# A hybrid state-space and pooling layer on one core: the z projection moved out of the state-space groups and made from seven block products per pair

## The chip, the cores and the metric

One Trainium2 chip, one of its cores. The metric is the device time of one execution in microseconds (us), as the median of several runs. A lower time is better. All inputs and outputs are fp32 tensors in the chip's memory.

## What is computed

One layer of a streaming encoder, for two request groups that share the weights: one prompt of 512 tokens and 8 samples of 16 tokens, together 640 tokens (`TOK`) with a model width of 1024. The reference, cut to the mixing sub-layer:

```python
u = rms_norm(x, g_pre_mix) * (1 + sc1) + sh1
proj = u @ w_in                                   # 1024 -> 9248
z, xbc, dt_raw, p, gates = jnp.split(proj, [2048, 6144, 6176, 7200], axis=-1)
xbc_c = jax.nn.silu(causal_dwconv(conv_hist, xbc, conv_w, conv_b))
xs, bm, cm = jnp.split(xbc_c, [2048, 3072], axis=-1)
dt = jax.nn.softplus(dt_raw + dt_bias);  a = -jnp.exp(a_log)
y, h_final = ssd_chunked(xs, dt, a, bm, cm, h0)   # 8 groups of 4 heads, state 128
y = y + xs * d_skip
yg = y.reshape(b, L, 2048) * jax.nn.silu(z)
yg = yg * lax.rsqrt(mean(yg * yg over the 256 columns of a group) + EPS)
y_ssd = (yg * g_ssd_norm) @ w_ssd_out
y_pool = multiscale_pool(p) @ w_pool_group * pool_scale
mix = (sigmoid(gate_a) * y_ssd + sigmoid(gate_b) * y_pool) @ w_o
x = x + gt1 * rms_norm(mix, g_post_mix)
```

The channel sub-layer follows: `w_up` (1024 to 4096), a squared ReLU, `w_down`. Inside `ssd_chunked` the decay of position l from position s is exp(min(a_cs[l] - a_cs[s], 0)), masked to s <= l. New states of the recurrence, the convolution and the pooling are outputs too.

## The kernel before

Activations lie transposed, features on the 128 partitions and the 640 tokens along the free dimension. Every large product is made in three fp32r matmuls: an operand is split in a high part (a cast on ACT, `S.copy`) and a low part (the rest, a subtraction on DVE), and hi*hi, lo*hi and hi*lo are added up in PSUM. `split` (lines 119 to 134) does this for one weight block of 128 x 1024, in rings of four `wh` and `wl` buffers. `fmm` (lines 154 to 162) makes one tile of 128 output features: 8 blocks of the inner dimension x 3 terms x 2 token regions, of 256 and of 384 tokens, so 48 matmuls with 320 columns on average, into one of two large PSUM buffers (`big`). Raw weights come in blocks of 1 MB through two `raw` buffers, loaded by SP's queue.

The stages in the order of the program:

- Prologue and pooling: conditioning, u, dt, the pooling branch `p` (tiles `pp`, `ypp`), and the first 2 of 16 gate tiles (`gate`, tiles `pga` and `pgb`; `gate_list`). The pooling branch's result goes to DRAM (`yp_d`), and a gate tile of the second half reads it back (`ypl`), multiplies, and writes `bf_d`. tanh of a gate tile lies in `tA`, the pooled rows in `tB`, two buffers each.
- State-space stage, 8 groups. `proj(g)` makes six tiles: four `px` (two of x, one of B, one of C; each followed by `conv_tile`, the width-4 convolution and its silu, in `L634` to `L646`) and two `pz` (`ztile`: tanh of half z on ACT, `L681`, then (tanh + 1) * z on DVE, `L682`, into `sz`). `ssd(g)` is the recurrence of a group in nine pieces; for each of five token tiles `common(t)` loads decay rows (`ab`, DMA by SP), transposes (`tp`), clamps with `pacs` on DVE (`M`, `L714`), takes four exp on ACT (`L716`, bias `nacs`), and PE makes `py` and `sp`. `sample_t`, `sample_a`, `sample_b` treat the 8 samples (`hTp`, `yo`, `ss`); `finish` multiplies by `sz` and sends `yg_d`; `finish2` sums squares (`ms`). `merge` lays `ssd(g-1)` between the tiles of `proj(g)`; in groups 2 to 5 the conditioning columns that are needed later (`ada`, `L301`, 1 MB of weights a step) lie among them too. `ssd(7)` lies between six gate tiles; eight gate tiles follow.
- Phase B: for each group one row of factors (`rb`) and two tiles (`yg`) are loaded by SP, multiplied (`L913`) and split (`put`, `L187` and `L188`) in `ynh` and `ynl`; then the tiles `pso` of `w_ssd_out`.
- Phase C and the channel sub-layer: `w_o` (`po`), v, then pairs of `w_up` tiles (class `Pair`, tiles `pq` and `pr`) and `w_down` (`pd`, `L1236`). A `Pair` makes two tiles from seven products of half size: the inner dimension, the two output tiles and the tokens (two halves of 320) are halved, sums of blocks are formed on DVE, and each product is 4 inner blocks x 3 terms = 12 matmuls of 320 columns (`L1185`), 84 in all. The first pair is made plainly (`L1169`), 96 matmuls of 320 columns.

The program is written in this order, and a scheduler at build time sets the order of each engine's queue; every queue (PE, ACT, DVE, POOL, and SP for DMA) then runs in order.

Of the kernel before, what the change touches and what calls it, by code (L numbers as in the profile page):

```python
# [60 lines left out]
def tile_hybrid_step(  # L61
# [36 lines left out]
    g_d = dp.tile([2, 9, 1024], F32, name="g_d")  # L98
    v_d = dp.tile([8, 128, 640], F32, name="v_d")
# [49 lines left out]
    PS0 = 256  # L149

    def reg(ps, g):
        return ps[:, 256:512] if g == 0 else ps[:, 512:896]

    def fmm(ps, w, act, ks, first, last, groups=(0, 1)):
        wh, wl = w
        (ah, al) = act
        n = len(ks)
        for i, (kw, ka) in enumerate(ks):
            for j, (ww, aa) in enumerate(((wh, ah), (wh, al), (wl, ah))):
                for g in groups:  # L160
                    T.matmul(reg(ps, g), ww[:, kw, :], aa[g][:, ka, :],  # L161
                             start=first and i == 0 and j == 0, stop=last and i == n - 1 and j == 2)
# [26 lines left out]

    def rsqrt(pool, m, shape, dst, tag):  # L190
# [25 lines left out]


# [12 lines left out]
    nacs = cp.tile([128, NT, 32], F32, name="nacs")  # L230
# [109 lines left out]
    uh, ul = act_views(256)  # L340
# [28 lines left out]
    def ada_cols(b):  # L369
# [213 lines left out]
    def gate(which, f):  # L583
# [5 lines left out]
        with tc.high_priority():  # L589
            S.activation(th, ps[:, PS0:PS0 + 640], AF.Tanh, scale=0.5)  # L590
# [35 lines left out]

    es_a = ExitStack()
    A = es_a.enter_context(tc.tile_pool(name="phaseA", bufs=1, reuse_waits="tile"))
    xcs, szs = {}, {}

    def conv_tile(ps, dst, ci, rc, slot):
        pv = ps[:, PS0:PS0 + 640].rearrange("p (b s) -> p b s", s=16)
# [7 lines left out]
        S.activation(ac, ps[:, PS0:PS0 + 640], AF.Identity, bias=colf[:, CB + ci:CB + ci + 1], scale=colw[:, 96 + ci:97 + ci])  # L640
# [7 lines left out]
    def proj(g):  # L648
# [3 lines left out]
        def xtile(i):  # L652
# [10 lines left out]
            conv_tile(ps, st["xc"][:, i, :], cols[i], st["rc"], i)  # L663

# [680 lines left out]
```

## Time and profile before

| | |
|---|---|
| median of 3 runs | 1366.09 us (1364.56 to 1368.3) |
| the profiled execution | 1366.78 us, its span 1365.0 us |
| PE busy | 1324.6 us, 97% of the span, 8940 matmuls |
| DVE, ACT, POOL busy | 892.8, 569.5, 90.7 us |
| moved by DMA | 192.25 MB, mean 141 GB/s |

A span runs from the first to the last instruction of the profile; what lies around it, 1.8 us here, is in the device time only. Busy time of PE counts overlapping matmuls, so a stage that is 100% busy can still hold short waits: how fast PE really goes is read from the start of one matmul to that of the next, or from the length of a whole tile. The granted clock is TensorE's, where 1.00 is 2.4 GHz and 0.50 is 1.2 GHz.

### The profile page before, as it was taken

What the parts mean: (1) busy time and instruction counts of PE and PEld (TensorE: products, weight loads), DVE (VectorE), ACT (ScalarE), POOL (GpSimd) and SP (SyncE); (2) the same over time, 40 slices, a digit from 0 to 9 for tenths busy, and PEclk for the clock granted to TensorE, in tenths of its full rate; (3) what the DMA queues carried; (4) which work ended last, traced back from release to release, by engine and by line L of the source; (5) the groups of instructions that cost most, each with busy time, mean ns of one, the idle gap of its engine ahead of it and who ended that gap; (6) DMA issues with size and microseconds to landing.
All of it is one profiled execution on the core that took longest, in us unless ns stands there. A gap on an engine that the chain in (4) does not pass through costs nothing.

```text
span 1365.0 us, 22238 instructions
## 1 busy us (share of the span) xinstructions
PE 1324.6 (97%) x8940; PEld 1195.8 (88%) x8940; DVE 892.8 (65%) x1729; ACT 569.5 (42%) x1097; POOL 90.7 (7%) x153
## 2 busy tenths in 40 slices
PE   4999999999999999999998999999999999999997
PEld 3999998878887889989898999779988988988886
DVE  4775667767776879686547333488745756667675
ACT  4444546454545555564334221365441422423331
POOL 0011011010201020102100000011000000000000
PEclk9999999999999999999999999999999999999999
DMA  9744524565546653435367633635212312212151
GB/s 298 224 112 125 157 84 125 148 216 187 167 147 214 181 180 93 130 105 173 103 205 267 211 100 132 216 122 187 93 62 63 104 51 93 93 55 100 62 201 47
DMA packets 134927, 192.25 MB, mean 141 GB/s; under 512 B 8541, under 2 KB 104877, under 8 KB 132776
## 3 DMA queue, kind: packets, MB, share of 16 engines
q1 hardware_dynamic: 123336, 160.96, 36.9%
q0 software_dynamic: 10016, 29.56, 6.9%
q8 instruction: 70, 1.15, 0.3%
q10 hardware_dynamic: 1472, 0.31, 0.1%
q14 instruction: 33, 0.27, 0.1%
HBM read 159.20 MB, written 31.60 MB: 140 GB/s over the span
## 4 chain that ended last, share of the span: by engine, by line
PE 84%; DMA 6%; DVE 4%; issue 3%; ACT 2%; ACTq 0%; POOL 0%; SPq 0%; DVEq 0%; POOLq 0%
PE pd L1236 16%; PE px L161 14%; PE pq L1185 8%; PE pz L161 8%; PE pso L161 8%; PE pga L161 4%; PE pr L1185 3%; PE po L989 3%; PE pp L161 3%; PE py L729 2%; DMA wz<-in_w_in_dram 2%; PE sp L748 1%; PE hTp L783 1%; PE yo L788 1%; PE pq L1169 1%
## 5 line engine op out<-in xcount | busy, mean ns | idle before, releaser
L161 PE MATMUL px<-AH,wh 128*128 128x256 f32 (+1 forms) x512 | 119.1, 314 | 0.0
L161 PE MATMUL px<-AH,wl 128*128 128x256 f32 (+1 forms) x512 | 117.9, 310 | 0.0
L161 PE MATMUL px<-AL,wh 128*128 128x256 f32 (+1 forms) x512 | 117.5, 310 | 0.0
L161 PEld LDWEIGHTS px<-AH,wh 128*128 128x128 f32 x512 | 91.5, 188 | 8.1 <-issue 4.6
L161 PEld LDWEIGHTS px<-AH,wl 128*128 128x128 f32 x512 | 93.0, 188 | 0.3 <-issue 0.3
L161 PEld LDWEIGHTS px<-AL,wh 128*128 128x128 f32 x512 | 93.1, 188 | 0.0
L1254 DVE TENSOR_TENSOR acc<-acc,pd 128x512 f32<-128x512 f32 (+1 forms) x61 | 40.7, 676 | 72.6 <-PE pd L1236 72.6
L1236 PE MATMUL pd<-wl,hh 128*128 128x512 f32 (+1 forms) x223 | 87.8, 394 | 0.2 <-DVE wl L133 0.2
L1236 PE MATMUL pd<-wh,hl 128*128 128x512 f32 (+1 forms) x223 | 87.7, 393 | 0.0
L1236 PE MATMUL pd<-wh,hh 128*128 128x512 f32 (+1 forms) x223 | 85.9, 392 | 0.0
L642 DVE SCALAR_TENSOR_TENSOR ac<-rw,colw,ac 128x640 f32<-128x640 f32 x96 | 84.3, 878 | 2.0 <-ACT ac L640 1.4
L161 PE MATMUL pz<-AH,wh 128*128 128x256 f32 (+1 forms) x256 | 62.4, 320 | 0.0
L161 PE MATMUL pz<-AH,wl 128*128 128x256 f32 (+1 forms) x256 | 61.4, 315 | 0.0
L161 PE MATMUL pz<-AL,wh 128*128 128x256 f32 (+1 forms) x256 | 60.3, 314 | 0.0
L716 ACT ACTIVATE M<-M,nacs 128x128 f32<-128x128 f32 x160 | 52.4, 397 | 17.0 <-DVE M L714 17.0
L161 PE MATMUL pso<-ynh,wh 128*128 128x256 f32 (+1 forms) x256 | 58.3, 309 | 0.0
L161 PE MATMUL pso<-ynh,wl 128*128 128x256 f32 (+1 forms) x256 | 58.3, 309 | 0.0
L161 PE MATMUL pso<-ynl,wh 128*128 128x256 f32 (+1 forms) x256 | 58.3, 309 | 0.0
L161 PEld LDWEIGHTS pz<-AH,wh 128*128 128x128 f32 x256 | 46.0, 188 | 6.8 <-issue 4.9
L1236 PEld LDWEIGHTS pd<-wl,hh 128*128 128x128 f32 x223 | 41.9, 188 | 9.7 <-DVE wl L133 0.6
L1236 PEld LDWEIGHTS pd<-wh,hl 128*128 128x128 f32 x223 | 42.0, 188 | 9.3
L1236 PEld LDWEIGHTS pd<-wh,hh 128*128 128x128 f32 x223 | 41.8, 188 | 8.8
(493 smaller groups left out, 3638.2 us busy)
## 6 DMA issues: line engine op xcount, KB each, us to landing
wada<-in_w_ada_dram SPq DMA_DIRECT2D x24, 1024.0 KB
wu<-in_w_up_dram SPq DMA_DIRECT2D x16, 1024.0 KB
wd<-in_w_down_dram SPq DMA_DIRECT2D x16, 1024.0 KB
ab<-acs_d SPq DMA_DIRECT2D x40, 256.0 KB
wxs<-in_w_in_dram SPq DMA_DIRECT2D x8, 1024.0 KB
wbc<-in_w_in_dram SPq DMA_DIRECT2D x16, 512.0 KB
wz<-in_w_in_dram SPq DMA_DIRECT2D x8, 1024.0 KB
h<-in_state_ssm_dram SPq DMA_DIRECT2D x16, 512.0 KB
```

Of the source, the lines that this page charges most:

```text
L161: T.matmul(reg(ps, g), ww[:, kw, :], aa[g][:, ka, :], start=first and i == 0 and j == 0, stop=last and i == n - 1 and j == 2)
L642: V.scalar_tensor_tensor(a3, rw[:, :, k:k + 16], colw[:, 32 * k + ci:32 * k + ci + 1], a3, ALU.mult, ALU.add)
L716: S.activation(M[:, hh, :], M[:, hh, :], AF.Exp, bias=nacs[:, t, 4 * g + hh:4 * g + hh + 1])
L729: T.matmul(py[64 * j:64 * (j + 1), 128 * qq:128 * (qq + 1)], xr[:, 2 * qq + j, :], M[:, 2 * qq + j, :], start=True, stop=stop)
L748: T.matmul(sp[:, 0:256], bt, xrd, start=True, stop=True)
L783: T.transpose(pt[:, 128 * b:128 * (b + 1)], st["h0"][qq][:, 4 * hb + b, :], ident)
L788: T.matmul(po[32 * c:32 * c + 32, o:o + 128], st["xc"][:, 3, 512 + 32 * c:512 + 32 * c + 32], hT[:, 2 * c + par, :], start=True, stop=True ...
L989: T.matmul(ps[:, HC[half]], aa[:, k, :], ww[:, HC[half]], start=k == 0 and j == 0, stop=k == 7 and j == 2)
L1169: T.matmul(ps[:, 512 * g:512 * g + HT], ww[:, k, :], aa[g][:, k, :], start=k == 0 and j == 0, stop=k == 7 and j == 2)
L1185: T.matmul(dst, ww[:, k, :], aa[:, k, :], start=start and k == 0 and j == 0, stop=stop and k == 3 and j == 2, skip_group_check=True)
L1236: T.matmul(ps, aa[:, k, :], ww[:, cols], start=first and k == 0 and j == 0, stop=last and k == n - 1 and j == 2)
L1254: V.tensor_tensor(acc[t][:, hc], acc[t][:, hc], ps, ALU.add)
```

## The change

- z leaves `proj`. A new class `Seven`, which also replaces `Pair`, makes the 16 z tiles as 8 pairs in a stage of their own between pooling and the state-space groups. For it u lies in two regions of 320 tokens (`HT`), the high and low parts of u are added up again (`uf`), four combinations of its quarters are formed and split (`UH`, `UL`), and four gate tiles are made ahead of the pairs. Each z tile, times tanh + 1 (or, negated, tanh - 1), goes to DRAM (`sz_d`) by POOL's queue, and `start` of a group loads it back by SP's.
- `proj` keeps the four `px` tiles; `ssd(7)` lies between four gate tiles instead of six, and six instead of eight follow.
- The clamp min(., 0) of the decay goes from DVE to ACT: relu of (pacs - ab) in four instructions, then one exp of the negative over all 512 columns. `nacs` goes.
- High and low parts of the pooled rows and of phase B's tiles lie in one row of 640 (`put_flat`): one cast and one subtraction each instead of two.
- The load of `yp_d` in a gate tile goes from SP's queue to POOL's.

```diff
-    def reg(ps, g):
-        return ps[:, 256:512] if g == 0 else ps[:, 512:896]
+    def reg(ps, g, n0):
+        return ps[:, 512 - n0:512] if g == 0 else ps[:, 512:1152 - n0]
...
+    def put_flat(pair, k, src):
+        h, l = pair
+        S.copy(h[:, k, :], src)
+        V.tensor_tensor(l[:, k, :], src, h[:, k, :].bitcast(F32), ALU.subtract)
...
+    class Seven:
...
+        def first(self):
...
+            self.x0 = split(self.r[:, :, 0:128], *KF)
+            with tc.high_priority():
+                V.tensor_tensor(s[:, 1], self.blk(2, 1), self.blk(2, 2), ALU.add)
+                V.tensor_tensor(s[:, 0], s[:, 1], self.blk(1, 1), ALU.add)
+            self.x1 = split(s, *KH)
+        def second(self):
...
+            self.x2 = split(self.z, *KH)
+            self.x3 = split(self.blk(2, 2), "p (k f) -> p k f", dict(k=4), n=512)
+        def run(self, nxt=None, late=None):
...
+            prod(A_, a11, b11, True)
+            S.copy(p1, A_)
+            prod(B_, sl(self.x1, 0), t2, True)
+            V.tensor_tensor(f1[:, HT:640], p1, B_, ALU.add)
+            prod(C_, sl(self.x1, 1), t1, True)
+            S.copy(f2[:, 0:HT], C_)
+            if nxt:
+                nxt()
+            prod(A_, a12, b21, False)
+            S.copy(f1[:, 0:HT], A_)
+            prod(B_, sl(self.x2, 0), t3, False)
+            V.tensor_tensor(f2[:, HT:640], p1, B_, ALU.add)
+            V.tensor_tensor(f2[:, HT:640], f2[:, HT:640], f2[:, 0:HT], ALU.add)
+            prod(C_, sl(self.x2, 1), b22, False)
+            V.tensor_tensor(f1[:, HT:640], f1[:, HT:640], C_, ALU.add)
+            self.tail(0, f1)
+            prod(B_, self.x3, t4, False)
+            V.tensor_tensor(f2[:, 0:HT], p1, B_, ALU.add)
...
         else:
             yp = tmp("tB", f"ypl{f}")
-            Y.dma_start(yp, yp_d[f])
+            G.dma_start(yp, yp_d[f])
...
+    for ks in (slice(0, 4), slice(4, 8)):
+        for g in range(2):
+            V.tensor_tensor(uf[:, ks, HT * g:HT * (g + 1)], uh[g][:, ks, :].bitcast(F32), ul[g][:, ks, :].bitcast(F32), ALU.add)
...
+    store_pair(q2, e22)
+    store_pair(q1, e11)
...
+    for f in range(4):
+        gate_list.pop(0)()
...
+            S.activation(th, f, AF.Tanh, scale=0.5)
+            V.scalar_tensor_tensor(f, th, -1.0 if i else 1.0, f, ALU.add, ALU.mult)
+            G.dma_start(sz_d[2 * g + i], f)
...
-        def ztile(i):
...
-            fmm(ps, split_k(st["r"], i), u, K8, True, True)
...
-            V.tensor_tensor(M, ab, pacs[:, t, hs].unsqueeze(2).broadcast_to([128, 4, 128]), ALU.min)
             for hh in range(4):
-                S.activation(M[:, hh, :], M[:, hh, :], AF.Exp, bias=nacs[:, t, 4 * g + hh:4 * g + hh + 1])
+                S.activation(M[:, hh, :], ab[:, hh, :], AF.Relu, bias=pacs[:, t, 4 * g + hh:4 * g + hh + 1], scale=-1.0)
+            S.activation(M, M, AF.Exp, scale=-1.0)
...
+            st["sz"] = A.tile([128, 2, 640], F32, tag="sz", name=f"sz{g}", bufs=2)
+            Y.dma_start(st["sz"], sz_d[2 * g:2 * g + 2].rearrange("i p n -> p i n"))
...
-    merge(gate_list[:6], ssd(7))
+    merge(gate_list[:4], ssd(7))
```

How the queues' order moves, at three places. The first is PE's queue where z is made: before, the end of group 0's last `px` tile and the start of its first `pz` tile.

```order
L161 MATMUL px_3_1756<-AL,wh 128x256
L161 MATMUL px_3_1756<-AL,wh 128x384
L161 MATMUL px_3_1756<-AH,wl 128x256
L161 MATMUL px_3_1756<-AH,wl 128x384
L161 MATMUL pz_0_1826<-AH,wh 128x256
L161 MATMUL pz_0_1826<-AH,wh 128x384
L161 MATMUL pz_0_1826<-AL,wh 128x256
L161 MATMUL pz_0_1826<-AL,wh 128x384
```

Now, in the first z pair, the end of its second product (`pqz_1796`), a part of its third (`prz_1797`), two matmuls of the next pair (`pqz_1925`), and its fourth:

```order
L269 MATMUL pqz_1796<-UH,wl 128x320
L269 MATMUL prz_1797<-UH,wh 128x320
L269 MATMUL prz_1797<-UL,wh 128x320
L269 MATMUL prz_1797<-UH,wl 128x320
L269 MATMUL pqz_1925<-AH,wh 128x320
L269 MATMUL pqz_1925<-AL,wh 128x320
L269 MATMUL pqz_1796<-AH,wh 128x320
L269 MATMUL pqz_1796<-AL,wh 128x320
L269 MATMUL pqz_1796<-AH,wl 128x320
```

A z tile was one run of 48 matmuls; a pair is now a chain of products that share two PSUM buffers, with a few matmuls of the next pair put between them.

The second place is PE's queue where the first group's recurrence ends (`hf` is the last prompt state's transpose, `tp_4`, `hTp` and `yo` are the samples' part). Before, it lies inside the next group's first `pz` tile:

```order
L161 MATMUL pz_0_2466<-AH,wl 128x256
L760 MATMUL hf_3_2381<-ident,hn_3_2378 128x128 x2
L702 MATMUL tp_4_2389<-ident,xc_1548 128x128 x3
L703 MATMUL tp_4_2389<-xc_1548 128x128
L783 MATMUL hTp_00_2411<-ident,h_0_2024 128x128 x4
L783 MATMUL hTp_01_2417<-ident,h_0_2024 128x128 x4
L161 MATMUL pz_0_2466<-AH,wl 128x384
L161 MATMUL pz_0_2466<-AH,wh 128x256
L161 MATMUL pz_0_2466<-AH,wh 128x384
L788 MATMUL yo_2409<-hT_0_2410,xc_1548 32x128 x2
```

Now it lies inside the next group's fourth and last `px` tile:

```order
L165 MATMUL px_3_3541<-AH,wh 128x320
L888 MATMUL hf_3_3459<-ident,hn_3_3456 128x128 x2
L830 MATMUL tp_4_3467<-ident,xc_2806 128x128 x3
L831 MATMUL tp_4_3467<-xc_2806 128x128
L913 MATMUL hTp_00_3489<-ident,h_0_3169 128x128 x4
L913 MATMUL hTp_01_3495<-ident,h_0_3169 128x128 x4
L165 MATMUL px_3_3541<-AH,wh 128x320
L165 MATMUL px_3_3541<-AL,wh 128x320
L918 MATMUL yo_3487<-hT_0_3488,xc_2806 32x128 x2
```

The same pieces of a group's recurrence stand between fewer tile matmuls, and the sums of squares (`ms`), which stood in the next group's first tile but one, now stand up to a tile later.

The third place is SP's queue at the start of phase B. Before, loads of pooled rows (`ypl`) stand among those of the factors and tiles:

```order
L867 DMA rs_d<-rsall_7680 5x128
L595 DMA ypl_7876<-yp_d 128x640
L907 DMA rb_8182<-rs_d 128x640
L912 DMA yg_0_8188<-yg_d 128x640
L912 DMA yg_1_8195<-yg_d 128x640
L907 DMA rb_8202<-rs_d 128x640
L912 DMA yg_0_8208<-yg_d 128x640
L912 DMA yg_1_8215<-yg_d 128x640
L595 DMA ypl_7935<-yp_d 128x640
L907 DMA rb_8222<-rs_d 128x640
```

Now none stands there, and the first two weight blocks of `w_ssd_out` stand ahead:

```order
L116 DMA wsa_8420<-in_w_ssd_out_dram 128x8x256
L980 DMA ms_d<-msr_7922 4x160
L994 DMA msall_7925<-ms_d 5x128
L116 DMA wsb_8422<-in_w_ssd_out_dram 128x8x256
L997 DMA rs_d<-rsall_7926 5x128
L1037 DMA rb_8308<-rs_d 128x640
L1042 DMA yg_0_8312<-yg_d 128x640
L1042 DMA yg_1_8317<-yg_d 128x640
L1037 DMA rb_8322<-rs_d 128x640
```

The loads of pooled rows moved to POOL's queue, where each stands behind the store of an earlier gate tile. From the second `pso` tile to the end PE's order is the same as before.

## Rows read from the trace of the kernel before

**Rows 1.** The page: PE's and DVE's busy time, and the granted clock by slice.
```profile
PE 1324.6 (97%) x8940; PEld 1195.8 (88%) x8940; DVE 892.8 (65%) x1729; ACT 569.5 (42%) x1097; POOL 90.7 (7%) x153
PEclk9999999999999999999999999999999999999999
```
**Rows 2.** The chain that ended last, in order of time: start us, us, what.
```profile
163.73 14.08 PE pz L161 x96
...
746.71 112.65 PE pso L161 x768
...
952.39 14.08 PE pq L1169 x96
...
1060.48 1.75 PE pq L1185 x12
...
1088.07 25.86 PE pd L1236 x111
```
**Rows 3.** Stretch with two pairs: us; busy PE, PEld, DVE, ACT, POOL; clock, DMA share, GB/s.
```profile
1060.48:1088.07 27.59, 27.59 (x179) 26.18 (x178) 21.01 (x31) 11.74 (x18) 0.00 (x0) 1.00 0.33 115
```
**Rows 4.** DVE in group 1's stretch, 177.67 to 236.82 us, by shape: busy, mean ns | idle before.
```profile
L714 DVE TENSOR_TENSOR M<-ab,pacs 128x512 f32<-128x512 f32 x5 | 3.4, 684 | 1.0 <-PE py L729 1.0
...
L133 DVE TENSOR_TENSOR wl<-wz,wh 128x1024 fp32r<-128x1024 f32 x2 | 2.4, 1216 | 0.0
...
L707 DVE TENSOR_TENSOR xr<-tp,dts 128x256 f32<-128x256 f32 x5 | 2.1, 419 | 5.1 <-PE tp L703 5.0
...
L682 DVE SCALAR_TENSOR_TENSOR sz<-tz,pz 128x640 f32<-128x640 f32 x2 | 1.6, 820 | 0.1
...
L133 DVE TENSOR_TENSOR wl<-wbc,wh 128x1024 fp32r<-128x1024 f32 x1 | 1.2, 1225 | 4.1 <-ACT wh L132 4.1
```
**Rows 5.** DVE's adds of 320 columns in the stretch of the two pairs.
```profile
L1210 DVE TENSOR_TENSOR rl<-rl 128x320 f32<-128x320 f32 x2 | 1.0, 484 | 0.0
```
**Rows 6.** Busy times in group 1, in group 2 with conditioning steps, and in a late stretch.
```profile
177.67:236.82 59.15, 59.15 (x454) 54.48 (x453) 44.71 (x96) 31.23 (x70) 7.35 (x12) 1.00 0.34 106
236.82:305.67 68.85, 67.57 (x510) 56.17 (x508) 47.17 (x99) 35.99 (x77) 7.35 (x12) 1.00 0.58 187
...
511.90:546.00 34.10, 34.10 (x272) 31.53 (x271) 31.09 (x65) 19.42 (x44) 0.73 (x1) 1.00 0.32 93
```
**Rows 7.** ACT in group 1's stretch, by shape.
```profile
L716 ACT ACTIVATE M<-M,nacs 128x128 f32<-128x128 f32 x20 | 6.7, 402 | 2.1 <-DVE M L714 2.1
...
L132 ACT CAST wh<-wz 128x1024 fp32r<-128x1024 f32 x2 | 2.1, 1046 | 6.1 <-PE px L161 6.1
...
L719 ACT ACTIVATE ab<-ab 128x512 f32<-128x512 f32 x3 | 1.9, 624 | 0.0
...
L681 ACT ACTIVATE tz<-pz 128x640 f32<-128x640 f32 x2 | 1.4, 702 | 0.1
```
**Rows 8.** Waits in groups 1 to 7: us in total, times, longest.
```profile
PE hf L760 <- DVE hn L755: 2.5, 2, 1.4
```
**Rows 9.** PE's timeline at the end of the gate tiles: start us, us [idle before].
```profile
737.84 0.56 PE L161 MATMUL pgb<-AH,wh 128*128 128x256 f32 x2 [4.78 <-ACT tgb L590]
```
**Rows 10.** Waits from 683 to 747 us: ACT's, and SP's own.
```profile
ACT ynh L187 <- DVE yg L913: 25.6, 11, 4.8
SPq L595 <- DMA bf_d<-ypl: 23.8, 4, 9.3
```
**Rows 11.** Clock and DMA in the first slice and in the two slices at phase B's start.
```profile
0.00:34.10 34.10, 14.88 (x204) 12.58 (x204) 14.62 (x43) 14.91 (x26) 2.52 (x8) 1.00 1.00 298
...
682.50:716.60 34.10, 34.10 (x239) 33.66 (x238) 17.02 (x32) 10.27 (x19) 2.20 (x4) 1.00 0.65 205
716.60:750.80 34.20, 29.40 (x189) 28.88 (x188) 26.21 (x44) 16.64 (x34) 2.16 (x4) 0.95 0.77 267
```
**Rows 12.** Timeline from the last group's sums to the last split of phase B's tiles.
```profile
684.47 0.52 SPq L850 DMA_DIRECT2D ms_d<-msr  x1
697.01 0.42 SPq L907 DMA_DIRECT2D rb<-rs_d  x1
746.82 0.89 DVE L188 TENSOR_TENSOR ynl<-yg,ynh 128x256 fp32r<-128x256 f32 x2
```

More of the change, by code (lines that the diff above doesn't have):

```diff
@@ L157, in fmm @@
         n = len(ks)
+        n0 = ah[0].shape[-1]
         for i, (kw, ka) in enumerate(ks):
@@ L188, in put, with groups @@
             V.tensor_tensor(l[g][:, k, :], src[:, sl], h[g][:, k, :].bitcast(F32), ALU.subtract)
+    def put_flat(pair, k, src):
+        h, l = pair
+        S.copy(h[:, k, :], src)
+        V.tensor_tensor(l[:, k, :], src, h[:, k, :].bitcast(F32), ALU.subtract)
+    def groups(pair):
+        return tuple([a[:, :, 0:256], a[:, :, 256:640]] for a in pair)
     def rsqrt(pool, m, shape, dst, tag):
@@ L218, in tile_hybrid_step, with store_pair, halves, chain @@
+    def store_pair(dst, src):
+        S.copy(dst[0], src)
+        V.tensor_tensor(dst[1], src, dst[0].bitcast(F32), ALU.subtract)
+    def halves(v):
+        return v[:, 0:4, 0:HT], v[:, 0:4, HT:640], v[:, 4:8, 0:HT], v[:, 4:8, HT:640]
+    def chain(pairs, k, after, late):
+        pairs[k].second()
+        pairs[k].run(nxt=after, late=late)
     es_c = ExitStack()
@@ L903, in tile_hybrid_step @@
     B = es_b.enter_context(tc.tile_pool(name="phaseB", bufs=1, reuse_waits="tile"))
-    ynh, ynl = [], []
+    yn = []
     for g in range(8):
@@ L913, in tile_hybrid_step @@
             V.scalar_tensor_tensor(yg, yg, colf[:, GSN + 2 * g + i:GSN + 2 * g + i + 1], rb, ALU.mult, ALU.mult)
-            put((hh, ll), i, yg)
-        ynh.append(hh)
-        ynl.append(ll)
+            put_flat((hh, ll), i, yg)
+        yn.append(groups((hh, ll)))
     mh, ml = act_views(256)
@@ new lines, in t_blocks, with up_pair, rows, tail @@
+        store_pair(t4, f21)
+        return lambda: store_pair(t3, f12)
+    def up_pair(e, fp):
+        def rows(i):
+            return rl_tile(e, 2 * fp + i)
+        def tail(i, f):
+            V.scalar_tensor_tensor(f, f, 0.0, f, ALU.min if i else ALU.max, ALU.mult)
+            put_hid(e, 2 * fp + i, f)
+        return Seven(f"u{e}{fp}", w_up[0], 512 * e + 256 * fp, Q, (b11, b21, b22, t1, t2, t3, t4), rows, tail)
+    def plain(p, e, fp):
+        for i in range(2):
+            ps = big(f"pq{p.n}{i}")
+            w = split_k(p.r, i)
+            for k in range(8):
+                for j, (ww, aa) in enumerate(((w[0], vh), (w[0], vl), (w[1], vh))):
+                    for g in range(2):
+                        T.matmul(ps[:, 512 * g:512 * g + HT], ww[:, k, :], aa[g][:, k, :], start=k == 0 and j == 0, stop=k == 7 and j == 2)
+            f = rl_tile(e, 2 * fp + i)
+            for g in range(2):
+                S.activation(f[:, HT * g:HT * (g + 1)], ps[:, 512 * g:512 * g + HT], AF.Relu)
+            V.tensor_tensor(f, f, f, ALU.mult)
+            put_hid(e, 2 * fp + i, f)
@@ L1269, in down @@
                     Y.dma_start(yout[t][:, hc], xr[t][:, hc])
-    pairs = {(e, fp): Pair(e, fp) for e in range(1, 8) for fp in range(2)}
+    pairs = {(e, fp): up_pair(e, fp) for e in range(1, 8) for fp in range(2)}
     P = [pairs[e, fp] for e in range(1, 8) for fp in range(2)]
@@ L1285, in tile_hybrid_step @@
     t3_late = t_blocks()
-    P[0].plain()
+    plain(P[0], 1, 0)
     t3_late()
```

198 lines of the change are left out of this document (85 added, 113 removed).

## The prediction

> **What bounds the kernel now.** I read the page first. PE is busy for 97% of the span, DVE for 65%, and the granted clock stands at 0.9 or more in every slice [rows 1]. So PE sets the time, and its matmuls run at the upper level, 2.4 GHz. The chain of waits says the same stage by stage: `pz`, `pso`, `pq` and `pd` follow each other with hardly anything between [rows 2]. The reader should see two unit prices there. A run of 96 matmuls of `pz` (regions of 256 and 384 columns) takes 14.08 us, and 96 matmuls of `pq` (two regions of 320) also take 14.08 us: 0.1467 us from start to start in both, so the new regions cost and give nothing, and a plain tile of 48 lasts 7.04 us. A product of 12 takes 1.75 us, the same pace.
>
> The sum is made against the profiled execution, 1366.78 us (span 1365.0 and 1.8 around it), 0.7 above the median. A difference under 0.3%, about 4.1 us, I count as no change.
>
> **Part 1, fewer matmuls.** Two z tiles cost 96 matmuls before, a pair costs 84: 8 pairs x 12 x 0.1467 = **-14.1 us**.
>
> **Part 2, waits inside the pairs.** Seven products in a chain share PSUM buffers with adds on DVE, so they may be longer than their matmuls. The stretch with two `w_up` pairs lasts 27.59 us with 179 records, so 11 beyond the 168 of the pairs [rows 3]. The strangers are `pd`, at 25.86/111 = 0.233 us each [rows 2]. That leaves (27.59 - 11 x 0.233)/2 = 12.5 us a pair, or 12.75 if only nine of them lie inside, against 84 x 0.1467 = 12.32. The wait is 0.2 to 0.43 us. z has no `pd` to fill holes with, only a few matmuls of the next pair, so I take 0.45: 8 x 0.45 = **+3.6 us** (bounds 1.6 and, if a pair gains nothing, 14.1).
> DVE must keep up. A 512-column operation takes 0.684, a 1024-column low part 1.22, the (tanh + 1) * z 0.82 [rows 4], a 320-column add 0.484 [rows 5]. A pair has four block sums and one short low part (5 x 0.684), three long low parts, five adds and two products: 3.4 + 3.7 + 2.4 + 1.6 = 11.1 us of some 12.75, 87%. In the late stretch DVE was at 31.09 of 34.10 us, 91%, and PE had no idle time [rows 6]. So it fits, narrowly.
>
> **Part 3, the start of the z stage.** `uf` and the combinations of u's quarters are some 12 DVE operations of 1280 columns, at 1.25 x 1.22 = 1.5 us each: 18 us. With the first pair's sums and the gate tiles' own splits DVE has about 27 us of work; the four gate tiles put ahead give PE 4 x 7.04 = 28.2 us. They cover it barely, if the pooling branch's memory is free in time. I take **+1.5 us** (0 to 5). Without that cover it would be the 18 us.
>
> **Part 4, state-space groups.** A plain group lasted 59.15 us, with DVE busy for 44.71 and ACT for 31.23 [rows 6]. Without its 96 `pz` matmuls PE needs 59.15 - 14.1 = 45.05 us. DVE loses the clamp (5 x 0.684), two low parts (2 x 1.216) and two products (2 x 0.820), 7.4 in all [rows 4]: 37.3 us remain, 83%. ACT loses two casts (2.1) and two tanh (1.4); 20 exp (6.7) become 20 relu of the same shape, and 5 exp of 512 columns come in at 0.624, 3.1 [rows 7]: 30.8 us, 68%. Neither is full. With the conditioning steps it is looser: DVE 47.17 - 7.4 = 39.8 of 68.85 - 14.1 = 54.8 us.
> But the pieces of a recurrence stand between two tiles fewer (the second order place in the section on the change), so a wait for DVE has less behind it. Group 1's DVE was idle for 14.4 us; 5.0 lay before `xr`, waiting for PE's `tp`, and 4.1 for ACT's cast [rows 4]. Now only 7.75 us of idling fit. The lower end: nothing waits, and the 2.5 us that PE waited for `hn` before `hf` in groups 1 to 7 [rows 8] go as well, -2.5. The upper end: all idling stays except the 1.1 us before the removed instructions, 13.3 - 7.75 = 5.6 us a group, +44. I take **+4 us**, half a microsecond a group, because the nearest row, the late stretch with DVE at 91% beside a full PE, lies far on the side of no wait.
> The chain of the clamp is no longer: min and four exp took 0.684 + 4 x 0.402 = 2.29 us, four relu and one exp 4 x 0.402 + 0.624 = 2.23.
> A rule speaks against this part: the Trainium skill ("ScalarE: Activation LUTs", Rules for kernel authors) says to put relu and min on VectorE, not on ScalarE. The rows agree on the price of the operation alone (0.684 against 1.6 us for 512 columns), and by the rule the 3.1 us more on ACT in each group would be time; the sum would then be 25 us higher.
>
> **Part 5, the hand-over to phase B.** Before, PE stood idle for 4.78 us in the last `pgb` tile, waiting for tanh `tgb` [rows 9]; ACT's queue was stuck behind `ynh`, which waited for `yg` on DVE, 25.6 us in 11 waits, and that for SP, whose queue waited 23.8 us in 4 waits before a `ypl` load for a buffer that `bf_d`'s store held [rows 10]. In that slice the clock was 0.95 [rows 11], a mix of the two levels: 0.05 x 34.2 = 1.7 us. With `ypl` on POOL's queue both should go: **-6.5 us**.
> The new wait: the last sums leave at 684.47, the first `rb` load at 697.01, and the last `ynl` ends at 747.7 [rows 12], 63.2 us of set-up. PE's cover was eight gate tiles, 56.3 us; now it is what remains of one tile and four more, 34.3. The first `pso` tiles need the last block only after 7/8 of a 14.08 us run, 12.3 us: 46.6 in all. The set-up without SP's 23.8 us is 39.4. By bytes: 24 + 10 rows of 320 KB, 2 MB of weights and 1 MB of states are about 14.3 MB; at the 298 GB/s of the first slice, where the DMA share is 1.00, they take 48 us [rows 11]. So between 0 and 63.2 - 46.6 = 16.6 us; I take **+3**, between the first two and nearer the rows with DMA at 1.00, since these slices ran at 205 and 267 GB/s with shares of 0.65 and 0.77.
> What the Trainium skill says here ("Perfetto Trace Analysis", Roofline) is a higher ceiling, about 435 GB/s for one core's 16 DMA engines; by it, as an estimate, the bytes take 33 us, no wait is left and the sum is 3 us lower. The first slice does not show that rate.
>
> **At nothing.** The z weights (16 blocks) and the stores and loads of gated z move from or to queues with room: 16 stores on POOL, which is busy for 7%, and loads of 640 KB a group needed only in `finish`, tens of microseconds later; DMA's share in a group was 0.34 [rows 6]. If such a load came late, `finish` and then `ms` would be late, at first under the next tile. `ypl` behind stores on POOL: one store, load and product of about 10 us for two tiles of 14.08; if it were longer, `tA` and `tB` would stop ACT's tanh. Flat rows: one call over 640 instead of two, on DVE (0.89 us for the pair before [rows 12]), off PE's path while the hand-over is covered.
>
> **The sum.** -14.1 + 3.6 + 1.5 + 4 - 6.5 + 3 = -8.5: 1358.3, and 0.7 less against the median, **1357.6 us**.
>
> **The rivals.**
> - *All hides.* Pair waits 1.6, nothing in parts 3 and 5, part 4 at -2.5: -14.1 + 1.6 - 6.5 - 2.5 = -21.5, so 1344.6. For it: DVE at 83% where 91% was borne. Against: all covers at once.
> - *The pairs do not save time.* The seven products wait so much that a pair lasts 14.08 instead of 12.77: 8 x 1.31 = 10.5 more, 1368.1, no change. For it: DVE at 87%, no `pd` between. Against: the `w_up` pairs do save.
> - *The recurrence sets the pace of the groups* (the other side). PE waits for DVE and ACT between the shorter row of tiles: before `tp`, `py`, `hf`, with ACT's relu queued for a free M buffer and all its casts behind. It decides from 9.8 us of DVE idling a group ((9.8 - 7.75) x 8 = 16.6, which is 12.6 over my 4). At 11 us it costs 3.2 x 8 = 25.8 instead of 4: 1379.4, slower. For it: 14.4 us of idling before, most of it not bound to z. Against: the idle time before `xr` waits for PE's tiles, and shrinks with them. The skill's rule above would come to nearly the same time, by ACT.
> - *The hand-over stays as long as it was*, 63.2 us: 16.6 instead of 3, so 1371.2, slower.
>
> **How the numbers follow.** Forecast 0.56 (its own range 1350 to 1364: faster 0.48, no change 0.08); all hides 0.10; pairs save nothing 0.10; groups paced by the recurrence 0.16; hand-over 0.08. Faster 0.48 + 0.10 = 0.58, no change 0.08 + 0.10 = 0.18, slower 0.24. The range leaves out the half of the first rival below 1344 and the half of the third above 1380, with a few in a hundred for the rest: 1344 to 1380.
>
> **What would show it.** z: a pair's start-to-start near 12.8 us, products (`pqz`, x12) of 1.75 to 2.0. Plain groups: 45 to 46 us with DVE near 37 and ACT near 31. No idle time before `pgb`; PE's wait before the eighth block of the first `pso` under 5 us; clock 0.9 or more throughout. From the second `pso` tile to the end, the same duration as before. I am wrong if a plain group lasts over 47 us, if a pair lasts over 13.5, or if the z stage begins with PE waiting for `UH` and `UL` for over 5 us.

## The result and the profile after

The changed kernel takes 1387.21 us in the median where the kernel before takes 1367.19 in the same measurement: a ratio of 1.0141, 95% interval 1.0123 to 1.016. It is **slower by 20 us**; the forecast was 1357.6, with a range up to 1380. One of the four runs behind the median took 2137.4 us at a granted clock of 0.56 and is not in the ratio. The profiled execution has a span of 1385.4 us, 20.4 more than before.

From the page of the changed kernel, the busy time of the engines and the granted clock by slice, which answer to [rows 1]:

```profile
PE 1328.4 (96%) x8844; PEld 1188.5 (86%) x8844; DVE 941.9 (68%) x1765; ACT 619.0 (45%) x1156; POOL 104.0 (8%) x177
PEclk9999999999999999999999999999999999999999
```

The 96 matmuls are gone (8844 for 8940) and yet PE is busy for 3.8 us more. The page hides the reason: a slice of 35 us with a clock of 0.91 still prints as a 9, and matmuls at the lower clock last longer (two `px` in a row 0.73 us at 525.73, 0.46 at 513.74) and count as busy. So the time is compared by stages, from the starts of the first matmuls of `pqz`, `px` and `pso` in PE's timelines (z before is 16 tiles at 7.04 us):

| stretch | before, us | after, us | difference |
|---|---|---|---|
| to the end of the pooling branch and the first gate tiles | 135.4 | 136.0 | +0.6 |
| four gate tiles (before they lie later) and 16 z tiles | 28.2 + 112.6 | 28.2 + 104.1 | -8.5 |
| groups, gate tiles, to the first `pso` (less z and those four gate tiles) | 611.1 - 140.8 = 470.3 | 494.0 | +23.7 |
| first 96 matmuls of `pso` | 14.1 | 19.4 | +5.3 |
| the rest | 604.4 | 603.8 | -0.6 |

(The last 12 matmuls of the last pair, 1.8 us, lie in the third row: the pairs really gained 6.7, the groups and gates lost 21.9.) The third row holds the loss. By windows over it, from the changed kernel (columns as in [rows 3]; a first, four groups with conditioning steps, a plain one, the first `pso` tiles):

```profile
298.30:341.80 43.50, 43.50 (x346) 39.40 (x345) 35.18 (x74) 29.09 (x68) 4.82 (x9) 1.00 0.27 84
341.80:405.30 63.50, 58.74 (x419) 44.19 (x417) 43.37 (x102) 38.67 (x85) 12.21 (x21) 0.97 0.58 177
405.30:459.60 54.30, 50.35 (x368) 42.79 (x369) 35.45 (x76) 26.26 (x57) 2.55 (x3) 0.91 0.65 207
459.60:525.00 65.40, 57.52 (x431) 44.55 (x429) 48.63 (x108) 41.83 (x95) 14.77 (x25) 0.97 0.62 189
525.00:575.50 50.50, 48.18 (x367) 40.73 (x368) 35.35 (x71) 26.63 (x54) 1.61 (x2) 0.97 0.70 209
...
613.00:661.40 48.40, 48.40 (x390) 42.40 (x388) 42.60 (x97) 35.54 (x82) 7.38 (x12) 1.00 0.52 156
...
762.20:781.60 19.40, 16.53 (x98) 15.59 (x97) 17.25 (x22) 9.04 (x12) 0.54 (x1) 0.91 1.01 356
```

Groups 2 to 5 take 233.7 us (63.5 + 54.3 + 65.4 + 50.5). Before, from 236.82 to 503.33, they took 266.5 with 56.3 of z in them: 210.2. That is 23.5 us, all of the loss. By group it is 8.8, 3.4, 11.3 and 0.1 us, so most of it lies in groups 2 and 4. Plain groups have next to no idle PE and a clock of 1.00; in the four with conditioning the clock stands at 0.91 to 0.97, where group 2 had 1.00 [rows 6]. The lower level, 1.2 GHz, is half of 2.4, so the clock's share is up to 0.03 x 63.5 + 0.09 x 54.3 + 0.03 x 65.4 + 0.03 x 50.5 = 10.3 us. PE's idle time in the four went from 3.9 us to 18.9, which is 15.0 more. The two overlap where PE was idle at the lower level; together they cover the 23.5.

What waits? The waits in the groups of the changed kernel, 268 to 661 us (total, times, longest):

```profile
ACT wh L133 <- DMA wbc<-in_w_in_dram: 16.6, 6, 4.4
...
ACT wh L133 <- DMA wxs<-in_w_in_dram: 12.0, 4, 4.5
...
PE py L857 <- DVE M L845: 7.8, 5, 3.2
...
PE px L165 <- ACT wh L133: 7.4, 4, 4.0
```

The same stretch, SP's own queue:

```profile
SPq L896 <- DMA yg_d<-sz: 53.6, 5, 17.9
SPq L903 <- DMA out_dram<-h: 46.1, 10, 11.0
SPq L116 <- PE ada L394: 40.0, 8, 12.9
```

ACT waits for weights to cast, PE for the casts (`M` stands behind a low part on DVE, which waits for such a cast). One place shows it. First SP's timeline of the changed kernel, then PE's, at the end of group 4's tiles:

```profile
515.25 0.38 SPq L116 DMA_DIRECT2D wxs<-in_w_in_dram  x1
518.89 0.33 SPq L116 DMA_DIRECT2D wada<-in_w_ada_dram  x1
```

```profile
514.12 1.90 PE L394 MATMUL ada<-wada,cT 128*32 128x512 f32 x10
...
517.78 1.06 PE L394 MATMUL ada<-wada,cT 128*32 128x512 f32 x6
520.07 0.92 PE L953 MATMUL ss<-bm,hl 64*128 64x512 f32 x3 [1.23 <-DVE h L956]
525.03 0.90 PE L165 MATMUL px<-AH,wh 128*128 128x320 f32 x2 [4.03 <-ACT wh L133]
```

The load of group 5's first weights (`wxs`) is issued at 515.25, right when PE has passed the first of two conditioning steps, and needed at once; PE gets it at 525.03. At the end of group 2 such a load comes 6 us ahead (399.10 for 405.34), at the ends of groups 3 and 5 26 and 27 us. Before, the load for the group that begins at 305.67 [rows 6] was issued 26 us ahead, behind a conditioning block too, but with both z tiles still to come:

```profile
279.50 0.33 SPq L115 DMA_DIRECT2D wada<-in_w_ada_dram  x1
279.93 0.39 SPq L115 DMA_DIRECT2D wxs<-in_w_in_dram  x1
```

Weights and conditioning blocks, 1 MB each, take turns in two `raw` buffers, so a block can be loaded only when the block two before it has been consumed. The conditioning list has 20 items, five to a group: 16 steps with a block each, and after every eight steps two closing items without a block. So groups 2 and 4 get five blocks, groups 3 and 5 three. Before, each tile of six had at most one item behind it, and the z block came between. With four tiles the five no longer fit: in groups 2 and 4 two steps stand together behind the last tile, and the next group's `wxs` waits for PE to pass the first of them. In the order of SP's queue in the changed kernel, for group 4 (other loads between left out):

```
L114 DMA wbc_5235<-in_w_in_dram 128x8x128 x2
...
L116 DMA wada_2_5394<-in_w_ada_dram 128x2048
...
L116 DMA wada_3_5535<-in_w_ada_dram 128x2048
...
L116 DMA wada_4_5549<-in_w_ada_dram 128x2048
...
L116 DMA wxs_5565<-in_w_in_dram 128x8x256
```

A second delay lies on top in SP's queue. The `wbc` loads of groups 2 to 4 stand behind loads of `sz` and `h`, and those wait for stores. In the chain that ended last (start us, us, what) group 2's `wbc` follows such a store:

```profile
349.44 6.63 DMA out_dram<-h
...
357.23 5.24 DMA wbc<-in_w_in_dram
```

PE had passed the step that held the buffer of this `wbc` by 354.2, so the queue cost up to 3 us more. The cast came late, `M` with it, and PE waited 3.1 us at 366 us.

### The profile page after: what moved, and what is told of

Its sections match the earlier page's. It is cut to its first block, busy times and chain, and to the rows that moved or that the text cites. A ratio compares the mean times of both kernels' runs of the same rounds, so it can differ in the third digit from the quotient of the medians.

```text
span 1385.4 us, 22244 instructions
## 1 busy us (share of the span) xinstructions
PE 1328.4 (96%) x8844; PEld 1188.5 (86%) x8844; DVE 941.9 (68%) x1765; ACT 619.0 (45%) x1156; POOL 104.0 (8%) x177
## 4 chain that ended last, share of the span: by engine, by line
PE 74%; DMA 10%; issue 6%; DVE 5%; ACT 3%; POOL 1%; SPq 1%; ACTq 0%; DVEq 0%; POOLq 0%
PE pd L1295 16%; PE px L165 11%; PE pqu L269 9%; PE pso L165 7%; PE pru L269 3%; PE pp L165 3%; PE po L1117 3%; PE pqz L269 3%; DMA wbc<-in_w_in_dram 2%; PE pga L165 2%; PE pgb L165 2%; PE py L857 2%; DMA wxs<-in_w_in_dram 1%; PE hTp L913 1%; PE sp L876 1%
## 5 line engine op out<-in xcount | busy, mean ns | idle before, releaser
L165 PE MATMUL px<-AH,wh 128*128 128x320 f32 x512 | 124.5, 320 | 7.4 <-ACT wh L133 7.4
L165 PE MATMUL px<-AH,wl 128*128 128x320 f32 x512 | 121.7, 316 | 0.4 <-DVE wl L134 0.4
L165 PE MATMUL px<-AL,wh 128*128 128x320 f32 x512 | 121.4, 314 | 0.0
L165 PEld LDWEIGHTS px<-AH,wl 128*128 128x128 f32 x512 | 86.1, 190 | 4.6 <-issue 3.9
L843 ACT ACTIVATE M<-ab,pacs 128x128 f32<-128x128 f32 x160 | 52.9, 394 | 42.4 <-PE py L857 40.4
L165 PE MATMUL pso<-ynh,wl 128*128 128x384 f32 (+1 forms) x256 | 58.9, 311 | 0.0
L133 ACT CAST wh<-Sau 128x1024 fp32r<-128x1024 f32 x10 | 10.5, 1051 | 87.8 <-DVE acc L1313 40.4
L165 PEld LDWEIGHTS pso<-ynl,wh 128*128 128x128 f32 x256 | 47.0, 190 | 3.0 <-DVE ynl L197 3.0
L165 PEld LDWEIGHTS pso<-ynh,wh 128*128 128x128 f32 x256 | 47.1, 190 | 0.8 <-ACT ynh L196 0.8
L165 PEld LDWEIGHTS pso<-ynh,wl 128*128 128x128 f32 x256 | 47.1, 190 | 0.0
```

What stands on the lines that cost most here:

```text
L133: S.copy(h, src)
L165: T.matmul(reg(ps, g, n0), ww[:, kw, :], aa[g][:, ka, :], start=first and i == 0 and j == 0, stop=last and i == n - 1 and j == 2)
L843: S.activation(M[:, hh, :], ab[:, hh, :], AF.Relu, bias=pacs[:, t, 4 * g + hh:4 * g + hh + 1], scale=-1.0)
```

## The experiments

Theory K is the turns of the two shared buffers. Rivals were S (SP's queue stands at the loads of `sz` and `h`), B (too many bytes for these groups' time), and R (the recurrence is too long for four tiles, the rival of the prediction). The first expectations speak of W, late weights in general: in the first run by S, in the second by K as well. In each run the kernel before was timed on the same chip; it stood between 1366.5 and 1367.8. The stretch from the first `px` to the first `pso` is quoted from PE's timeline beside the medians (changed kernel: 494.0).

**The load of sz later in the program.**

```diff
         def start():
-            Y.dma_start(st["sz"], sz_d[...])
         def sample_a():
+            Y.dma_start(st["sz"], sz_d[...])
```

> The load of a group's gated z moves from the group's start to just before it is used, so that the queue of SP no longer stands at it ahead of the loads of states and of the next weights. Theory W (the changed kernel loses about 23 us in groups 2 to 5 because SP's queue stands at the sz load for the store of an earlier group, 53.6 us in 5 waits, and the wbc weights behind it come late): 1365 to 1379, with the yg_d<-sz wait gone from SP's queue and the waits px<-wh and py<-M in groups 2 to 5 smaller. Theory R (the recurrence is too long for the shorter row of tiles, whatever the queue does): 1384 to 1391, as the changed kernel, 1387.2.

1385.8 us, ratio 1.0151 (1.0124 to 1.0178): as the changed kernel. But the scheduler put the load nearly where it had been. SP still waited for `yg_d` 35.9 us in 3 waits in groups 2 to 4, where the changed kernel had 36.3, so the run decides nothing.

**The conditioning steps in the z stage.** Two or three items behind each pair, none in the groups.

> The conditioning steps (16 blocks of 1 MB) move from groups 2 to 5 into the z stage. Theory W, in the form that the two raw buffers and SP's queue are shared by weights and conditioning blocks: groups 2 to 5 come down to the length of plain groups, 23 us are won there, and the z stage (75 GB/s of weights) takes the blocks with a loss of 0 to 8: 1364 to 1373. Theory R: groups 2 to 5 lose as much as plain groups would for a recurrence that is too long; only the steps' own time moves: 1383 to 1391.

1374.71 us, 1.0054 (1.0036 to 1.0072), just above W's range and far below R's. A group in the middle and its neighbour:

```profile
421.40:466.50 45.10, 45.10 (x357) 39.75 (x357) 39.41 (x88) 31.73 (x72) 7.33 (x12) 1.00 0.53 157
466.50:512.80 46.30, 46.17 (x366) 40.57 (x365) 38.98 (x88) 32.73 (x74) 7.35 (x12) 1.00 0.53 153
```

Without conditioning a group takes what the prediction gave it (45.05 us; DVE 37.3, ACT 30.8). **R is refuted**: the recurrence fits four tiles. The stretch falls to 451.7; of the 42.3 us, 15.9 are the steps themselves (from the start of each of their 128 matmuls to PE's next one, in the kernel before) and 26.4 the loss. (SP's queue stood at `sz` and `h` here too, for 32.9 and 49.7 us.) But the z stage grows from 104.1 to 134.3, 14 more than the steps' own time.

**The clamp back on DVE.**

```diff
+            V.tensor_tensor(M, ab, pacs[...], ALU.min)
             for hh in range(4):
-                S.activation(M[:, hh, :], ab[:, hh, :], AF.Relu, bias=pacs[...], scale=-1.0)
-            S.activation(M, M, AF.Exp, scale=-1.0)
+                S.activation(M[:, hh, :], M[:, hh, :], AF.Exp, bias=nacs[...])
```

> The clamp of the decay goes back to DVE (one min over 512 columns, four exp with a bias on ACT), everything else as changed. Theory R in the form that ACT's 3.1 us more a group hold up PE: 1375 to 1383. Theory W: the clamp costs nothing as long as weights come late: 1384 to 1392.

1389.36 us, 1.0176 (1.0153 to 1.0199). No gain, and the interval overlaps that of the change. The Trainium skill ("ScalarE: Activation LUTs", Rules for kernel authors) would have the clamp on VectorE; here, with 1389.4 against 1387.2 us, the engine that makes it does not matter.

**z made plainly**, 48 matmuls a tile, no block sums, in the same stage.

> The 16 z tiles are made plainly in the same stage, 48 matmuls each, without block sums and without the combinations of u. The trace of the changed kernel shows 106 us for the eight pairs where 16 plain tiles take 112.6, so both theories: 1391 to 1396, slower than the changed kernel by 4 to 9 us. If the pairs' gain were lost by a later start of the groups, the same as the changed kernel within 2 us.

1398.71 us, 1.0241 (1.0223 to 1.0258), 11.5 above the change. z takes 112.6 us as it should; another 3.8 us lie behind the groups, in the first 96 `pso` matmuls (20.6 us) and after them (606.3), and were not followed up. The seven products are worth at least the 6.7 us of the table.

**Conditioning items spread out**, four to a group over groups 2 to 6, and three to a group over groups 1 to 7.

```diff
-    AD = {2: a1[:5], 3: a1[5:], 4: a2[:5], 5: a2[5:]}
+    al = a1 + a2
+    AD = {g: al[4 * g - 8:4 * g - 4] for g in range(2, 7)}
```

> The 20 items of the conditioning steps are spread four to a group over groups 2 to 6, one behind each of the four tiles, where the changed kernel has five to a group over groups 2 to 5, so that two stand together behind the last tile. Theory K (raw blocks share two buffers; with two conditioning blocks in a row ahead of the next group's first weights, SP can load those weights only when PE has consumed the last but one, and no tile is left to cover the load): most of the 23 us that groups 2 to 5 lose come back, 1366 to 1376. Theory S (SP's queue stands at the sz and h loads, whatever the conditioning does): 1383 to 1390. Theory R (the recurrence is too long for four tiles): 1383 to 1390.

1382.95 us, 1.0117 (1.0101 to 1.0134); the stretch 484.8. Four to a group gives back only a part, less than K expected. PE's idle time in the stretch fell from 20.5 to 8.4 us, but the conditioning matmuls now took 31.6 us for 28.4.

> The same 20 items three to a group over groups 1 to 7. Theory K: as with four to a group or a few us better, 1364 to 1374; if it is the bytes of a group that count (DMA as a rate), also better than four to a group by 2 to 6. Theories S and R: 1383 to 1390.

1373.0 us, 1.0041 (1.0025 to 1.0057); the stretch 479.7. Two of its groups:

```profile
447.50:497.80 50.30, 50.09 (x398) 42.01 (x397) 40.74 (x93) 33.18 (x77) 7.40 (x12) 1.00 0.58 186
497.80:550.20 52.40, 50.81 (x391) 41.48 (x390) 40.22 (x88) 32.79 (x74) 7.37 (x12) 1.00 0.63 195
```

The clock is back at 1.00, and SP's queue waited 120.9 us in 11 waits for `h` stores, where the change had 46.1, and the stretch still fell by 14.3 us: against S as the main cause. B fits as well as K here.

**The load of sz on POOL's queue.**

```diff
-            Y.dma_start(st["sz"], sz_d[...])
+            G.dma_start(st["sz"], sz_d[...])
```

> The load of gated z goes to POOL's queue, behind the store that it waits for; SP's queue no longer holds it (in the run that wrote it later in the program, SP's queue stood at it as before, 35.9 us in 3 waits in groups 2 to 5, so that run did not try the theory). Theory S: 1367 to 1379, and no yg_d<-sz wait in SP's queue. Theory K: at most a few us, 1382 to 1388.

1398.82 us, 1.0232 (1.0209 to 1.0255): 11.6 slower than the change, outside both expectations. The wait for `yg_d` left SP's queue. POOL's queue, where the stores of `h` now stand behind the `sz` loads, waited 14 us at them, and SP's waited longer for `h` (66.0 us for 46.1) and for the sums (34.2 for 5.6); that the one made the other was not shown. SP's queue, 268 to 660 us:

```profile
SPq L903 <- DMA out_dram<-h: 66.0, 11, 23.2
SPq L116 <- PE ada L394: 36.9, 7, 13.3
SPq L980 <- ACT msr L979: 34.2, 3, 23.1
```

S in this form gave the wrong sign; the waits for conditioning matmuls stayed.

**The load of pooled rows back on SP's queue.**

> The load of pooled rows in a gate tile goes back to SP's queue. If the removed idle time at the hand-over (6.5 us before) was due to that load standing in SP's queue, it comes back: 1391 to 1396. If the changed order alone took it away, or the six gate tiles hide the load, 1385 to 1389.

1391.13 us, 1.0173 (1.0158 to 1.0189), 3.9 above the change, all in the first 96 `pso` matmuls: 24.0 us there for 19.4, the clock 0.86 for 0.91.

```profile
761.50:785.50 24.00, 17.49 (x97) 16.53 (x98) 19.85 (x25) 9.78 (x13) 1.08 (x2) 0.86 0.92 315
```

**Same bytes, same groups, another place.** In groups 2 and 4 two blocks stand between the first and second tile, one behind the last.

```diff
-            main = [z for p in zip(main, AD[g] + [None] * 9) for z in p if z] + AD[g][len(main):]
+            main = [main[0], d[0], d[1], main[1], d[2], main[2], d[3], main[3], d[4]]
```

> Five conditioning items a group over groups 2 to 5, as in the changed kernel, so the same bytes in the same groups; only the place of the doubled block moves: two blocks stand between the first and the second tile, and one behind the last (changed: one behind each of the first three, two behind the last). Theory K (it is the two conditioning blocks in a row right ahead of the next group's first weights that leave no tile to cover their load): 1370 to 1378. Theory B (the bytes of these groups, 1 MB a block through two buffers, are too many for their time, wherever the blocks stand): 1383 to 1391.

1376.34 us, 1.0068 (1.0041 to 1.0094), 11 below the change; the stretch 483.2. The same blocks in the same four groups, and half of the loss is gone. The `wxs` loads at the ends of groups 2 and 4 now come 14 and 12 us ahead, where they came 6 and 10 ahead and PE still waited 4. **B does not explain it; K does.** Its six runs spread from 1371.9 to 1382.9.

**Eight steps in the z stage, two items a group**, in the shared buffers.

> Eight conditioning blocks, one behind each z pair, the other twelve items two to a group over groups 1 to 6. The run with three to a group still has its groups 1 to 7 some 10 us above PE's work; the run with all items in the z stage won 22 us in the groups and lost 15 there, with two and three blocks in a row. Theory B (bytes for the time at hand): both stages stay under their rate, 1362 to 1369. Theory K alone: no block stands beside another, so as good, 1362 to 1369; if a z pair loses 1 us and more for each block, 1370 to 1376.

1394.58 us, 1.0196 (1.0177 to 1.0214): slower than the change, against both. The z stage is 130.0 us, 26 longer for eight steps, and the groups with two items still hold a stretch of 475.9. The expectation was wrong on both theories. Two items a group instead of three bring next to nothing over the run with three, so bytes alone do not set this. By K, one conditioning block between two weight blocks makes each weight block wait for the weights before it; that is a reading after the fact, tried below.

**One edit alone in the kernel before**: `ypl` on POOL's queue.

> The kernel before with one edit of the change, the load of pooled rows in a gate tile on POOL's queue. If the 6.5 us of idle time and low clock at the hand-over came from that load in SP's queue: ratio to the kernel before 0.994 to 0.997. If eight gate tiles hide everything but the tanh wait and that has another cause: 0.998 to 1.002.

1.0002 (0.9993 to 1.0012): nothing. The slice at phase B's start kept its clock of 0.95 [rows 11], and the first 96 `pso` matmuls took 15.7 us for 14.1.

```profile
716.00:751.00 35.00, 30.64 (x197) 30.15 (x197) 27.27 (x43) 15.94 (x32) 4.87 (x9) 0.95 0.83 285
```

**Own buffers for the conditioning blocks**: the temporary tiles of the gate stage, idle during the groups; five items a group over groups 2 to 5 as in the change, then three over groups 1 to 7.

```diff
-                st["w"] = raw(w_ada[0, 128 * k:128 * (k + kr), c0:c0 + 4 * n]...)
+            for cg in range(4):
+                w = tmp("tA" if cg % 2 == 0 else "tB", f"wada{name}_{k}_{cg}")[:, 0:n]
+                Y.dma_start(w, w_ada[0, 128 * k:128 * (k + 1), c0 + n * cg:c0 + n * (cg + 1)])
```

> The conditioning blocks leave the two 1 MB buffers that they share with the weights: each step is loaded in four pieces of 256 KB in the temporary tiles of the gate stage, which lie idle then. Same steps, same groups (five items a group over groups 2 to 5), same bytes. Theory K (turns of two shared buffers: a weight block waits until the block two before it is consumed): the groups lose their waits and their low clock, 1360 to 1372. Theory B (bytes of these groups against DMA's rate): 1382 to 1392. Theory S (the sz and h loads at the head of SP's queue): 1380 to 1390.

1378.48 us, 1.0076 (1.0059 to 1.0093), 8.7 below the change, with the stretch at 484.5: between K's expectation and B's. In its groups ACT no longer waits for a weight block, nor PE for a cast. Of PE's waits from 164 to 790 us, these two lie in the groups, beside 0.7 us at `ms` and 0.5 at `adaT`:

```profile
PE ada L387 <- DMA wada<-in_w_ada_dram: 4.6, 3, 3.1
...
PE py L856 <- DVE M L844: 0.3, 1, 0.3
```

SP still stands at `h` (30.8 us) and `sz` (24.8), less than in the change. The scheduler now set group 2's `wbc` load (344.29) ahead of them, so S keeps a share that this run does not separate. A group's window, and the sum over groups 1 to 5 from 298 to 563 us:

```profile
511.13:566.89 55.76, 55.33 (x401) 42.44 (x398) 41.68 (x93) 34.84 (x83) 7.90 (x13) 1.00 0.67 210
...
sum 265.00, PE 259.96 PEld 205.85 DVE 198.30 ACT 163.05 POOL 35.88; mean PE 51.99 PEld 41.17 DVE 39.66 ACT 32.61 POOL 7.18
```

PE is idle for 5.0 us there, where the change had 18.9, and the clock stays at 1.00 over the whole stretch: with the buffers apart most of the waits and all of the low clock are gone, with the same blocks in the same groups. **That is against B and for K.** What is left is a new cost: each piece has its own matmul, and the four of a step stand apart. The 128 conditioning matmuls take 32.9 us of PE's time (start to next start, 3.6 of it waits) where they took 15.9 before and 28.4 in the change (7.6 of it waits).

> The same own buffers, with the items three to a group over groups 1 to 7. Theory K: as own5 or up to 4 us better, 1358 to 1369, and below the kernel before (1367.4) if the 14 us that the run with three to a group still lost are turns of the buffers too. Theory B: as the run with three to a group in shared buffers, 1371 to 1376.

1370.7 us, 1.0025 (1.0014 to 1.0035), above K's range and just below B's; conditioning matmuls 22.7 us.

> As own3 (own buffers, three items a group over groups 1 to 7), but the four pieces of a step are loaded one step ahead, so that its four matmuls can stand together: in own3 and own5 they stood apart, and the conditioning matmuls took 22.7 and 32.9 us of PE's time from start to start against 16.9 in the run with shared buffers and three to a group. Theory K with that price: 1364 to 1368, at or below the kernel before; if the price of own buffers is the smaller pieces themselves, 1369 to 1373.

1370.11 us, 1.0016 (1.0006 to 1.0027), in the range of the price of smaller pieces. No step gained: the scheduler still set one matmul of four apart, and the sum stayed at 22.7 us. In the stretch PE is idle for 0.7 us and the clock is 1.00, yet it takes 476.3 us for the 470.3 before: the conditioning matmuls (22.7 for 15.9) and the samples' `ss` matmuls (19.3 for 14.5, start to next start) cost more where they stand now. This is the best form of the change found, and it only comes within 0.3% of the kernel before: **no version is faster than the kernel before**.

> Own buffers, loaded a step ahead, with eight steps in the z stage (one behind each pair) and twelve items two to a group over groups 1 to 6. With shared buffers this arrangement gave 1394.6, and its z stage was 25 us longer than without conditioning. Theory K (in shared buffers, one conditioning block between two weight blocks makes each weight block wait for the one before it): the 25 us shrink to 4 to 10, 1362 to 1372. Theory B or a z stage that has no room beside its pairs: 1380 to 1395.

1378.74 us, 1.0079 (1.006 to 1.0098), between the two ranges. Own buffers take 16 us off the arrangement that was slowest, 11 of it in the stretch (464.6 for 475.9). The z stage only falls from 130.0 to 126.1, still 22 longer for eight steps, so its loss is not the buffers' turns for the most part. The steps' 64 matmuls hold 12.8 us of it, more idle time of PE 4.3 and the low clock up to 3.4; why stays open.

## Why the prediction was wrong

The step that failed is one sentence of part 4: "With the conditioning steps it is looser: DVE 47.17 - 7.4 = 39.8 of 68.85 - 14.1 = 54.8 us." It looked at an engine's busy time. What sets the pace there is how long before its use a weight block can be loaded. Taking out z took out a weight block and two tiles between the blocks, and the same five conditioning items were then laid over four tiles. The order of the changed queue shows three `wada` in a row ahead of a `wxs`, and the trace of before shows such a load issued 26 us ahead; neither was priced. Of the 28.9 us between the forecast (-8.5) and the spans (+20.4), 23.5 lie in groups 2 to 5, 3.8 in the pairs and 2.3 at the first `pso`.

- *Part 1*, -14.1: right, 96 matmuls fewer.
- *Part 2*, +3.6: undersized. A pair takes (104.1 + 1.8)/8 = 13.2 us, not 12.77, so it loses 0.9 us, 7.4 in all. The z stage as a window: DVE is busy for 81.63 of 106.6 us, 77% where I had 87%, so its load was not the limit. PE is idle for 2.8 us, at most 1.3 at a time, for ACT's copy of a product. The rest, 4.5 us, lies in 43 matmuls after which the next starts 0.20 to 0.31 us later instead of 0.147.

```profile
164.00:270.60 106.60, 103.80 (x678) 99.18 (x677) 81.63 (x113) 49.55 (x72) 8.12 (x15) 1.00 0.39 128
```

- *Part 3*, +1.5: nothing. The first `pqz` follows the last gate matmul without a gap.
- *Part 4*, +4: plain groups about as worked out (45.1 us in the run without conditioning in the groups, DVE 2 us and ACT 1 us higher). In the changed kernel groups 1, 6 and 7 took 43.5, 37.5 and 48.4 us; the last is over my sign of 47, but 84 `py` matmuls lie in it where a group has 68. Groups 2 to 5 lost 23.5 us, of which the clock holds up to 10.3, a term that I put only into the hand-over. In the rival's condition (9.8 - 7.75) x 8 is 16.4, not 16.6.
- *Part 5*, -6.5 and +3: half. The new wait was 5.3 us. The 6.5 us at the last gate tile did go: PE is idle for 1.4 us in all the late gate tiles and the clock is 1.00. But that `ypl` on SP had cost them was argued, not shown, and the run with that edit alone gives nothing: the idle time shrinks at the last gate tile and comes back at the first `pso`. In the changed kernel the same edit is worth 3.9 us; that the shorter cover makes the difference is argued. The 298 GB/s that I took for a ceiling was none: the first `pso` tiles saw 356 GB/s at a share of 1.01. The Trainium skill's figure ("Perfetto Trace Analysis", Roofline), about 435 GB/s for one core's 16 DMA engines, is above both.
- *At nothing*: SP did stand at `sz`, 53.6 us in 5 waits, which I had not foreseen. With the waits at `h` it held up `wbc` loads, on top of the buffers' turns; how much of the 23.5 us this is was not separated.

Of the rivals, the one on the slower side named the right places (PE waits for `M` and casts) and the wrong reason: it put the limit in the recurrence, and in every group. That the loss sits in groups with conditioning, and most of it in the two with five blocks, is what tells the two apart.

The sum by stages is -6.7 (z) + 0.6 + 21.9 (groups and gates) + 5.3 - 0.6 = 20.5, and the spans differ by 20.4. K is shown by two runs: double blocks moved, -11; own buffers, -8.7, with PE's idle time down from 18.9 to 5.0 us and no low clock, against a cost of some 17 us over before in the conditioning matmuls. How the 23.5 us divide between the buffers' turns, SP's waits at `sz` and `h` and the clock was not separated.

## What to carry to other kernels

When work is taken out between two consumers of one small ring of buffers, recount for every block how long before its use its buffer comes free, and compare with load, cast and subtraction together (here 8.7 + 1.05 + 1.2 us): an engine's busy share says nothing of it. Before a waiting load moves to another queue, look at what will stand behind it there: `sz` on POOL's queue cost 11.6 us. A list that was fitted to six slots must be fitted again to four; spreading it evenly cost one line and gave back 14 of 20 us.

## What was not expected of the hardware

- In groups 2 to 5 of the changed kernel the granted clock fell to its lower level four times, for 20.5 us in all. Each fall came during a wait of PE of 0.8 to 4.0 us or 1.5 us after one; two to four waits are listed in each of these groups. With the steps three to a group it fell in none of the groups, though waits of 1.0 to 1.9 us were left, and with own buffers a wait of 3.1 us left it at 1.00. What decides was not tried.
- The conditioning matmuls, which fill 32 of 128 columns each, cost by how they stand: 128 of them took 15.9 us with the four column groups of a step together, about 1 us a step, and 32.9 us (3.6 of it waits) when they stood apart, with the clock at 1.00.
- 1 MB took 8.66 us from issue to landing when it was needed at once (`wxs` at 515.25, on the chain of waits), beside stores of 640 and 512 KB and another load of 1 MB. The first half of a `wbc`, 512 KB, had taken 7.04 us:

```profile
418.79 7.04 DMA wbc<-in_w_in_dram
...
515.25 8.66 DMA wxs<-in_w_in_dram
```
